# Output norms of the head groups: when the last scaling of a norm comes, and what the outgoing products wait for

## The chip, the cores and the metric

The kernel runs on one core of a Trainium2 chip. PE (TensorE) multiplies and transposes, DVE (VectorE), ACT (ScalarE) and POOL (GpSimd) work on elements, SP (SyncE) issues most of the transfers. Each engine takes its own instructions in the order in which the program records them, and waits for the others by semaphores. The metric is the time of one execution on the device in microseconds (us), as the median of several runs.

## The reference

One layer of a streaming encoder is computed for 1024 prompt tokens and 32 sample tokens. In the mix part, which the change touches, an input projection feeds two groups of heads: stick-breaking attention (8 heads of 64) and HGRN2 (4 heads of 128, a gated linear recurrence). Each head's output is normed on its own, and both go through one outgoing product:

```python
x = x + 0.5 * swiglu(rms_norm(x, ffn1_norm), ffn1_w_in, ffn1_w_out)
h = rms_norm(x, mix_norm)
sq, sk, sv, hq, hf, hi, hg = jnp.split(h @ w_in, IN_SPLIT_POINTS, axis=-1)
...
sb_o = rms_norm(sb_mix(sq, sk, sv), sb_out_gain).reshape(B, T, SB_WIDTH)
...
x = x + concat(normA(attnA), gatednormB(hgrnB)) @ w_out
x = x + 0.5 * swiglu(rms_norm(x, ffn2_norm), ffn2_w_in, ffn2_w_out)
```

(The last line but one is the docstring's wording; the sample tokens also read cached keys and values and a carried state.)

## The kernel before

Everything lies with channels on the 128 partitions and tokens along the row: T is 1056 columns, 1024 of the prompt and 32 of the sample, cut into three pieces of 384, 384 and 288 (TG is 384). A float32 product is made of three passes over high and low halves; `split` (L158 on ACT, L159 on DVE) makes these halves.

**The head groups.** Four head groups run one after the other, each of two attention heads and one HGRN2 head. For each there are three generators: `attend_stream` (prompt attention), `sample_stream` (attention of the 32 sample tokens) and `hg_stream` (the HGRN2 scan). A fourth generator, the products, runs beside all of them: first `project_stream` (L882, tile `pp`), the input projections of all groups, then `mix_stream` (L1520, tile `ps`), the outgoing products.

**What sets the order.** `merge` takes, again and again, the stream that stands at the earliest place and lets it record its next step. A step yields a cost; `Stream.advance` adds it up and turns the share of the stream's total (ATTEND_COST, SAMPLE_COST, HG_COST, or 412 units for the products) into a place. A stream that yields None waits, and the next one in line records a step. One unit of the products is six matmuls of a block. So the order of the instructions on every engine is fixed when the program is made; nothing is chosen on the chip, apart from what a scheduler of the program adds.

**Output norms.** Each head stream ends with a norm of its output, in blocks of TG columns, by `skewed`: first `factors` of block 0, then `factors` of block 1 and the scaling `normed` of block 0, and so on, with the last block's scaling alone at the end. `factors` squares the output on ACT (tile `sq`), transposes the squares on PE (`pmc`, L217), sums them per token and head on DVE (L218, tiles `fo` for attention and `fh` for the scan), and takes the power -1/2 on POOL (L224). `normed` spreads these factors over the rows again: for attention ACT widens them first (`wide`, L236), then PE transposes them (`pb`, L244), and DVE multiplies the output by them (L1096 for attention, tiles `so` and, for the sample tokens, `sos`). Prompt attention has three blocks, the scan three, the sample tokens one.

**Where outputs go.** In groups 0 to 2 the scaled output is stored to a DRAM tensor `mixd` (tiles c0, c1, c2 of it for attention and c4, c5, c6 for the scan); in group 3 it is split straight into operands (`xs_b`). `mix_stream` begins by loading the six tiles of `mixd` one after the other into `mraw` (L1481), in the two buffers `qn` and `kn` in turn (c0, c2 and c5 share one, c1, c4 and c6 the other), and splits each into `xs_a`. Its products then read `xs_a` in the order c0, c1, c2, c4, c5, c6. It may record these loads as soon as the last keys are done (`dup_done[3]`), once the projections have been recorded; a load of a part of `mixd` waits for the stores into it that were recorded ahead of it.

Of the kernel before, what the change touches and what calls it, by code (L numbers as in the profile page):

```python
# [1070 lines left out]
def skewed(first, second, items):  # L1071

    items = list(items)
    for i in range(len(items) + 1):
        if i < len(items):
            first(items[i])
            yield 1.0
        if i:
            second(items[i - 1])
            yield 0.5  # L1080


def sb_out_norm(g, pool, psp, o, w, out):
    nc = g.nc
    f = {}

    def factors(c):
        cw = min(TG, w - c)
        sq = g.wp.tile([P, TG], F32, name="sq", tag="xp", bufs=3)
        nc.scalar.activation(sq[:, 0:cw], o[:, c:c + cw], AF.Square)  # L1090
        f[c] = pool.tile([P, 3, 2], F32, name="fo", tag="fo", bufs=3)
        token_factors(g, f[c], psp, sq, cw, g.filler)

    def normed(c):
        cw = min(TG, w - c)
        nc.vector.scalar_tensor_tensor(out=o[:, c:c + cw], in0=o[:, c:c + cw], scalar=g.og[:, 0:1],  # L1096
                                       in1=spread(g, psp, f[c], 0, cw), op0=ALU.mult, op1=ALU.mult)
        out(c, c + cw, o[:, c:c + cw])

    yield from skewed(factors, normed, range(0, w, TG))  # L1100


def step_cost(w):
    return (w + 256) / 512.0


def attend_parts():

    for h in range(2):
        for p in range(4):  # L1110
            for a in ((0,) if p < 2 else (512, 0)):
                for i in (2 * p, 2 * p + 1):
                    yield h, p, a, i, min(a + 512, (i + 1) * P)


ATTEND_COST = sum(step_cost(e - a) for _, _, a, _, e in attend_parts()) + 12.0


def attend_stream(g, m, pool, psp, gi, out):
# [230 lines left out]
def hg_stream(g, m, pool, psp, hh, state, outs, out):  # L1350
# [108 lines left out]
    def normed(n):  # L1459
# [4 lines left out]
        out(*GROUPS[n], o[:, gs(n)])  # L1464

    yield from skewed(factors, normed, range(NG))
    m.scanned[hh] = True

# [5 lines left out]
def mix_stream(g, m, psp, xs, mix, xd):  # L1474

    nc = g.nc
    while not m.dup_done[3]:
        yield None
    for i, c in enumerate(MIX_FIRST):
        raw = m.sp.tile([P, T], F32, name="mraw", tag=("qn", "kn")[i % 2], bufs=1)  # L1480
# [147 lines left out]
def tile_layer(ctx: ExitStack, tc: tile.TileContext, *aps):  # L1628
# [207 lines left out]
    def products():  # L1836
        yield from project_stream(g, psp, xs_mix, jobs)
        m.projected = True
        yield from mix_stream(g, m, psp, xs_mix, mix, xd)

    def attention(gi):
        yield from attend_stream(g, m, m.sp, psp, gi, to_xs(3) if gi == 3 else to_dram(gi))
        finish()

    def sample(gi):
        yield from sample_stream(g, m, m.sp, psp, gi, ck, cv, to_xs(3) if gi == 3 else to_dram(gi))
        finish()
# [20 lines left out]
    for gi in range(4):  # L1868
        t0 = 7.0 * gi
        end = PLACES_END if gi == 3 else PLACES  # L1870
        streams.append(Stream(attention(gi), ATTEND_COST, *(t0 + t for t in end[0])))
        streams.append(Stream(sample(gi), SAMPLE_COST, *(t0 + t for t in end[1])))
# [103 lines left out]
```

## Time and profile before

| | |
|---|---|
| median of 3 runs | 2154.57 us (2151.69 to 2154.62) |
| the profiled execution's own time | 2158.07 us |
| its span, first to last instruction | 2156.4 us |
| mean granted TensorE clock | 0.996 |
| PE busy in 700 to 1450 us, where the head groups run | 735.50 of 750 us |
| head groups 0, 1, 2 end at about | 922, 1077, 1231 us |
| last input projection, last loads of `mraw` | about 1307 us, 1317 us |

The profile is of one execution. A group row gives the busy time of an engine and the mean of one instruction; a timeline row gives start and length, and in brackets how long the engine had stood idle before it and which instruction released it. In a row of stretches the last three numbers are the granted clock of TensorE, the share of the DMA engines, and GB/s.

### The profile page before, as it was taken

The page shows a single profiled execution, that of the slowest core. Times are in us where ns is not written, and L with a number is a line of the kernel's source. Part 1 is how long each engine was busy: PE and PEld are TensorE (multiplying, and loading weights), DVE is VectorE, ACT ScalarE, POOL GpSimd, SP SyncE. Part 2 cuts the span into 40 slices and gives each one's busy share as a digit, 9 for nine tenths or more (in the row PEclk, how much of TensorE's full clock was granted, in tenths as well). Part 3 has the DMA queues.
Part 4 walks back from the last instruction along what each step waited for, and adds up shares of the span by engine and source line. Part 5 has one row for each costly group of instructions (what it writes and reads, how often), then busy time and mean ns, then how long its engine had stood idle before and what let it go on. Part 6 is the DMA issues. An engine that isn't in the chain of part 4 may idle for free.

```text
span 2156.4 us, 41445 instructions
## 1 busy us (share of the span) xinstructions
PE 2107.1 (98%) x16331; PEld 2056.6 (95%) x16331; DVE 1470.4 (68%) x2546; ACT 937.8 (43%) x1820; POOL 590.7 (27%) x873
## 2 busy tenths in 40 slices
PE   7999999999999999999999999999999999999998
PEld 7999999999999999989899898999999999999998
DVE  5877666664678658778678688559677666645775
ACT  6433233233446555555564565246233233334443
POOL 1355544341000111311311311031565454320000
PEclk9999999999999999999999999999999999999999
DMA  7665555547535320120121122465765555566343
GB/s 230 188 204 176 156 166 168 160 140 265 204 123 169 117 59 21 44 70 21 55 60 29 60 68 92 147 192 160 226 210 173 165 164 162 165 231 231 120 144 125
DMA packets 327076, 305.12 MB, mean 141 GB/s; under 512 B 26400, under 2 KB 283168, under 8 KB 326880
## 3 DMA queue, kind: packets, MB, share of 16 engines
q1 hardware_dynamic: 257728, 262.59, 37.6%
q10 hardware_dynamic: 68672, 38.25, 6.2%
q8 instruction: 128, 2.10, 0.4%
q0 software_dynamic: 480, 1.62, 0.2%
q14 instruction: 68, 0.56, 0.1%
HBM read 207.37 MB, written 95.03 MB: 140 GB/s over the span
## 4 chain that ended last, share of the span: by engine, by line
PE 81%; DMA 7%; DVE 5%; POOL 2%; issue 2%; ACT 2%; SPq 0%; ACTq 0%; DVEq 0%; POOLq 0%
PE bk L431 33%; PE bk L746 20%; PE pp L882 14%; PE ps L1520 2%; PE pl L1391 2%; PE av L1158 1%; PE pt L1139 1%; DMA oraw<-in_ffn_w_out_dram 1%; DMA wraw<-in_ffn_w_in_dram 1%; DMA gd<-gt 1%; PE bk L799 1%; PE z L1194 1%; DMA p<-pd 1%; PE ps L1547 1%; PE z L1193 1%
## 5 line engine op out<-in xcount | busy, mean ns | idle before, releaser
L746 PE MATMUL bk<-tl,wh 128*128 128x256 f32 x1232 | 350.1, 285 | 1.0 <-DVE tl L704 0.9
L746 PE MATMUL bk<-th,wl 128*128 128x256 f32 x1232 | 349.2, 284 | 0.0
L746 PE MATMUL bk<-th,wh 128*128 128x256 f32 x1232 | 348.0, 284 | 0.7 <-ACT th L703 0.7
L882 PE MATMUL pp<-xs_a,wh 128*128 128x384 f32 (+1 forms) x1008 | 258.4, 338 | 0.0
L746 PEld LDWEIGHTS bk<-tl,wh 128*128 128x128 f32 x1232 | 231.8, 188 | 1.8 <-DVE tl L704 1.6
L746 PEld LDWEIGHTS bk<-th,wh 128*128 128x128 f32 x1232 | 230.9, 188 | 1.2 <-ACT th L703 1.0
L746 PEld LDWEIGHTS bk<-th,wl 128*128 128x128 f32 x1232 | 231.8, 188 | 0.2 <-issue 0.2
L882 PEld LDWEIGHTS pp<-xs_a,wh 128*128 128x128 f32 x1008 | 168.6, 189 | 6.1 <-issue 4.1
L693 DVE SCALAR_TENSOR_TENSOR wl<-oraw,wh 128x1024 fp32r<-128x1024 f32 x84 | 96.0, 1142 | 107.8 <-ACT wh L692 107.8
L882 PE MATMUL pp<-xs_a,wl 128*128 128x384 f32 (+1 forms) x504 | 163.9, 325 | 0.0
L586 POOL TENSOR_TENSOR gt<-gt,b 128x256 f32<-128x256 f32 x88 | 74.4, 846 | 316.4 <-ACT gt L585 316.4
L692 ACT ACTIVATE wh<-oraw 128x1024 fp32r<-128x1024 f32 x84 | 83.7, 997 | 148.6 <-PE bk L746 126.5
L159 DVE TENSOR_TENSOR wl<-wraw,wh 128x512 fp32r<-128x512 f32 (+2 forms) x126 | 110.7, 893 | 34.1 <-ACT wh L158 33.8
L585 ACT ACTIVATE gt<-gt 128x256 f32<-128x256 f32 x88 | 37.2, 423 | 219.3 <-DVE gt L552 219.2
L431 PE MATMUL bk<-ops_a,wh 128*128 128x256 f32 (+1 forms) x704 | 130.2, 285 | 2.2 <-ACT e L411 2.2
L158 ACT ACTIVATE wh<-wraw 128x512 fp32r<-128x512 f32 (+2 forms) x126 | 89.5, 731 | 91.2 <-PE bk L431 27.5
L590 POOL TENSOR_TENSOR gt<-gt,b 128x256 f32<-128x256 f32 x88 | 89.4, 1016 | 81.7 <-DVE b L552 69.1
L431 PEld LDWEIGHTS bk<-ops_a,wh 128*128 128x128 f32 x704 | 108.8, 188 | 2.8 <-ACT e L411 2.8
L552 DVE TENSOR_TENSOR gt<-bk,p 128x256 f32<-128x256 f32 (+1 forms) x60 | 25.9, 432 | 109.1 <-PE bk L431 106.3
L431 PE MATMUL bk<-ops_a,wl 128*128 128x272 f32 (+1 forms) x352 | 99.9, 285 | 0.3 <-DVE wl L159 0.3
L882 PEld LDWEIGHTS pp<-xs_a,wl 128*128 128x128 f32 x504 | 94.7, 188 | 0.1
L1050 ACT ACTIVATE t<-z,minus 128x128 f32<-128x128 f32 (+2 forms) x96 | 55.4, 577 | 62.8 <-PE z L1196 48.5
(437 smaller groups left out, 6559.5 us busy)
## 6 DMA issues: line engine op xcount, KB each, us to landing
wraw<-in_ffn_w_in_dram SPq DMA_DIRECT2D x58, 512.0 KB, 4.2
oraw<-in_ffn_w_out_dram SPq DMA_DIRECT2D x94, 256.0 KB, 4.6
sd<-osum SPq DMA_DIRECT2D x44, 512.0 KB, 3.1
gd<-gt SPq DMA_DIRECT2D x42, 528.0 KB, 5.0
braw<-in_ffn_w_in_dram ACTq DMA_DIRECT2D x42, 512.0 KB, 4.4
oraw<-sd SPq DMA_DIRECT2D x40, 512.0 KB, 3.8
oraw<-in_ffn_w_out_dram SPq DMA_DIRECT2D x30, 512.0 KB, 3.4
wraw<-in_w_in_dram SPq DMA_DIRECT2D x28, 512.0 KB, 3.7
```

The lines of the kernel that those rows point to most:

```text
L158: nc.scalar.activation(hi, src, AF.Copy)
L159: return nc.vector.tensor_tensor(out=lo, in0=src, in1=hi, op=ALU.subtract)
L431: mm = g.nc.tensor.matmul(ps, wt[x][:, kk, :], xt[y][:, kk, :], start=(first and kk == 0 and n == 0), stop=(kk == HK - 1 and n == len(PASS ...
L586: nc.gpsimd.tensor_tensor(out=gt[:, 1, cc], in0=gt[:, 1, cc], in1=s["b2"], op=ALU.mult)
L590: last = nc.gpsimd.tensor_tensor(out=gt[:, 0, cc], in0=gt[:, 0, cc], in1=s["b1"], op=ALU.mult)
L692: nc.scalar.activation(h, r, AF.Copy, scale=0.5)
L693: nc.vector.scalar_tensor_tensor(out=l, in0=r, scalar=0.5, in1=h, op0=ALU.mult, op1=ALU.subtract)
L746: nc.tensor.matmul(ps, wt[a][:, d * P:(d + 1) * P], xt[b][:, cols(c)], start=(k == 0 and n == 0), stop=(k == FH - 1 and n == len(PASSES) - 1))
L882: g.filler = nc.tensor.matmul(ps[:, 0:gw(n)], wt[a][:, k, :], xs(b, k)[:, gs(n)], start=(k == 0 and j == 0), stop=(k == KC - 1 and j == le ...
L1050: nc.scalar.activation(a, z, AF.Sigmoid, scale=minus)
L1391: nc.tensor.matmul(pl[0:rows, c, 0:hl].rearrange("p (b m) -> p b m", m=m_), k[:, cs(b, c)][:, 0:rows], qr, start=True, stop=True)
L1520: nc.tensor.matmul(ps[:, 0:w], wt[a][:, k, :], xs(b, c)[:, gs(n)], start=(k == 0 and i == 0), stop=(k == 5 and i == len(PASSES) - 1))
```

## The change

`skewed` gets one more step ahead of the last scaling: it yields 2.0 units, so that other streams record their steps first. ATTEND_COST grows by the same 2.0; the totals of the sample streams and of the scan stay as they were (10 and 24). `mix_stream` now waits, beside `dup_done[3]`, until all outputs of the first three groups have been recorded as done (`attended`, `sampled`, `scanned`).

```diff
@@ -1076,6 +1076,8 @@
             first(items[i])
             yield 1.0
         if i:
+            if i == len(items):
+                yield 2.0
             second(items[i - 1])
             yield 0.5
 
@@ -1113,7 +1115,7 @@
-ATTEND_COST = sum(step_cost(e - a) for _, _, a, _, e in attend_parts()) + 12.0
+ATTEND_COST = sum(step_cost(e - a) for _, _, a, _, e in attend_parts()) + 14.0
 
@@ -1474,7 +1476,7 @@
 def mix_stream(g, m, psp, xs, mix, xd):
 
     nc = g.nc
-    while not m.dup_done[3]:
+    while not (m.dup_done[3] and all(m.attended[:3] + m.sampled[:3] + m.scanned[:3])):
         yield None
```

No instruction of the computation is added or taken away. Lines behind 1078 stand two further down in the new kernel (L1520 becomes L1522, L1096 becomes L1098, and so on).

On PE at the end of head group 2, before (`pb<-identr,wide` belongs to prompt attention, `pb<-identr,fh` to the scan):

```order
L217 MATMUL pmc<-identr,sq 128x128 x3
L882 MATMUL pp<-xs_a,wh 128x384 x2
L882 MATMUL pp<-xs_a,wl 128x384
L882 MATMUL pp<-xs_b,wh 128x384
L244 MATMUL pb<-identr,wide 128x128 x3
L882 MATMUL pp<-xs_b,wh 128x384
L882 MATMUL pp<-xs_b,wl 128x384
L244 MATMUL pb<-identr,fh 128x128 x3
L882 MATMUL pp<-xs_a,wh 128x384
L244 MATMUL pb<-identr,wide 128x128 x2
```

And after the change, at the same place:

```order
L217 MATMUL pmc<-identr,sq 128x128 x3
L244 MATMUL pb<-identr,fh 128x128 x3
L217 MATMUL pmc<-identr,sq 128x128 x3
L1195 MATMUL z<-KH,Q 128x128
L244 MATMUL pb<-identr,fh 128x128 x3
L1196 MATMUL z<-KL,Q 128x128
L1198 MATMUL z<-cmask,identr 128x128
L882 MATMUL pp<-xs_a,wh 128x384 x2
L244 MATMUL pb<-identr,wide 128x128 x2
L882 MATMUL pp<-xs_a,wl 128x384
```

The attention's last `pb` stands further behind its `pmc`, and the scan's `pmc` and `pb` stand next to each other, with little between them.

On SP, where the outputs are loaded again, before (`mraw<-mixd` are the loads, `mixd<-sos` stores the sample tokens' scaled output of group 2, `xp` are tiles of the residual):

```order
L1481 DMA mraw<-mixd 128x1056
L1227 DMA craw<-in_cache_sb_k_dram 128x4x128
L1232 DMA vnew<-vsd 32x128
L1481 DMA mraw<-mixd 128x1056
L174 DMA wraw<-in_w_out_dram 128x3x128 x2
L1805 DMA mixd<-sos 128x32
L1481 DMA mraw<-mixd 128x1056 x2
L1487 DMA xp<-xd 128x384 x2
L1481 DMA mraw<-mixd 128x1056 x2
```

And after the change:

```order
L1483 DMA mraw<-mixd 128x1056
L1229 DMA craw<-in_cache_sb_k_dram 128x4x128
L1234 DMA vnew<-vsd 32x128
L1483 DMA mraw<-mixd 128x1056
L174 DMA wraw<-in_w_out_dram 128x3x128 x2
L1483 DMA mraw<-mixd 128x1056 x2
L1807 DMA mixd<-sos 128x32
L1489 DMA xp<-xd 128x384 x2
L1483 DMA mraw<-mixd 128x1056
L174 DMA wraw<-in_w_out_dram 128x3x128 x2
L1489 DMA xp<-xd 128x288
L1483 DMA mraw<-mixd 128x1056
```

The store of `sos` has moved behind the third and fourth load (these are now c4 and c6); the two loads behind it are c2, which it writes a part of, and c5.

On DVE after the change, from the scaling of `sos` on (L159 with `mraw` is the low half of a split; `hk`, `hq`, `att`, `hf` at L1403 to L1411 are a level of the scan of group 3):

```order
L159 TENSOR_TENSOR xs_a<-mraw,xs_a 128x1056
L159 TENSOR_TENSOR sbl<-pt,sbh 128x4x128
L1375 TENSOR_TENSOR att<-pd,identr 128x512
L1098 SCALAR_TENSOR_TENSOR sos<-sos,og,pb 128x32
...
L159 TENSOR_TENSOR xs_a<-mraw,xs_a 128x1056
L218 TENSOR_REDUCE fo<-pmc 128x6
L1403 TENSOR_TENSOR hk<-hk,hf 128x512
L1405 TENSOR_TENSOR hq<-hq,hf 128x512
L1410 COPY_PREDICATED att<-lmask_3097,pl 128x512
L1411 TENSOR_TENSOR hf<-hf 128x512
L159 TENSOR_TENSOR xs_a<-mraw,xs_a 128x1056
```

The scaling of `sos`, which stood ahead of every split of `mraw`, now comes behind the split of c4; the last row, c2's split, stands behind the four rows of the scan's level.

## The prediction, on record before the changed kernel was run

> **What bounds the kernel now.** I read the page's busy shares first, then the PE waits of the stretch between 730 and 1400 us in which the four head groups run, then the timelines of the places where the change moves something.
>
> ```profile
> PE 2107.1 (98%) x16331; PEld 2056.6 (95%) x16331; DVE 1470.4 (68%) x2546; ACT 937.8 (43%) x1820; POOL 590.7 (27%) x873
> ```
>
> PE is the bound: every other engine has a third of the span free. The change neither adds nor removes a matmul, so only PE's idle time (and its clock) can move the end. In the stretch that it touches, the largest waits of PE are these (total us, times, longest):
>
> ```profile
> PE pb L244 <- ACT wide L236: 4.2, 4, 1.5
> PE ps L1520 <- DVE xs_a L159: 1.1, 2, 0.7
> PE pmc L217 <- DVE fh L218: 0.6, 2, 0.3
> ```
>
> The first row is what the change aims at: `pb` spreads the token factors of an output norm over the rows, right before the last scaling of that norm. Three of the four are the ends of head groups 0, 1 and 2 (columns: start, us, instruction, idle before it):
>
> ```profile
> 922.29 0.44 PE L244 MATMUL pb<-identr,wide 128*128 128x128 f32 x2 [1.19 <-ACT wide L236]
> 1077.01 0.44 PE L244 MATMUL pb<-identr,wide 128*128 128x128 f32 x2 [1.51 <-ACT wide L236]
> 1231.40 0.44 PE L244 MATMUL pb<-identr,wide 128*128 128x128 f32 x2 [1.27 <-ACT wide L236]
> ```
>
> Together 3.97 us. That is little: 0.18% of the kernel, just under the 0.2% (4.3 us) that a measurement of this kernel can tell from no change. All else depends on what the move costs elsewhere.
>
> **Part 1: ends of groups 0 to 2.** The end of group 2, engine by engine:
>
> ```profile
> 1228.02 0.86 POOL L224 TENSOR_TENSOR fh<-fh,mh 128x3 f32<-128x3 f32 x1
> 1229.29 1.61 POOL L224 TENSOR_TENSOR fo<-fo,mh 128x4 f32<-128x4 f32 x1
> 1230.93 0.41 ACT L236 ACTIVATE wide<-fo 128x256 f32<-128x256 f32 x1 [3.94 <-POOL fo L224]
> ```
>
> POOL's power of the last `fo` ends at 1230.90, ACT widens it until 1231.34, PE goes on at 1231.40. With the attention's last `pb` behind some 5 us more of other products, this wait goes in all three groups: 4.0 us. Half of the `pmc` waits (0.6) go too: 0.3. But the scan's own norm uses the same helper, and there the order now sets `pmc` and its `pb` closer for the middle block. What that chain takes by itself stands at the end of group 3:
>
> ```profile
> 1406.32 0.55 PE L217 MATMUL pmc<-identr,sq 128*128 128x128 f32 x3 [0.98 <-ACT sq L1453]
> 1406.91 0.55 DVE L218 TENSOR_REDUCE fh<-pmc 128x3 f32<-128x384 f32 x1
> 1407.83 0.85 POOL L224 TENSOR_TENSOR fh<-fh,mh 128x3 f32<-128x3 f32 x1
> 1408.74 0.60 PE L244 MATMUL pb<-identr,fh 128*128 128x128 f32 x3 [0.74 <-POOL fh L224]
> ```
>
> `pmc` to `pb` needs 1408.74 - 1406.32 = 2.42 us. In the new order 1.0 to 1.4 us of PE work stands between the two, so about 1.05, 1.1 and 1.4 us of wait come up in the three groups, 3.55 in all. Net: 3.55 - 4.3 = **-0.7 us**. Bounds: -4.3 if other rows cover the new waits, +1.4 if only 0.5 us of work lies in each (3 x 1.9 - 4.3).
>
> **Part 2: the handoff to the outgoing products, around 1297 to 1340 us.** Here is the price. Sample attention of group 2 has one block only, so its only scaling is also its last: it is put off past the end of the projections. Now:
>
> ```profile
> 1298.16 0.24 DVE L1096 SCALAR_TENSOR_TENSOR sos<-sos,og,pb 128x32 f32<-128x32 f32 x1
> 1298.43 0.34 SPq L1805 DMA_DIRECT2D mixd<-sos  x1
> 1306.89 3.76 SPq L1481 DMA_DIRECT2D mraw<-mixd  x2
> 1317.03 1.45 SPq L1481 DMA_DIRECT2D mraw<-mixd  x2
> ```
>
> The store of `sos` leaves at 1298.43, long before the third load of `mraw` (output tile c2, into which `sos` goes) at 1306.89. In the new order DVE has the scaling behind the split of c4, and SP the store behind four loads; c2's load must wait for the store, and c5's load for c2's slot. I lay this chain out on the clock of the trace.
>
> ```profile
> 1310.00:1320.00 10.00, 9.30 (x61) 7.85 (x59) 9.91 (x14) 6.06 (x12) 0.91 (x4) 1.00 0.49 157
> mraw<-mixd SPq DMA_DIRECT2D x6, 528.0 KB, 3.3
> mixd<-sos SPq DMA_DIRECT2D x3, 16.0 KB, 1.4
> L158 ACT ACTIVATE xs_a<-mraw x6: 1074/1087/1119, 1303.8 to 1322.8; 128x1056 fp32r<-128x1056 f32 x6
> L159 DVE TENSOR_TENSOR xs_a<-mraw,xs_a x6: 1247/1255/1259, 1305.6 to 1323.9; 128x1056 fp32r<-128x1056 f32 x6
> ```
>
> (The first row gives the busy time of PE, PEld, DVE, ACT and POOL in a stretch: DVE is busy for 9.91 of its 10 us, so nothing on it comes early.) From the first split at 1305.6 on, the rows of DVE up to and with the scaling sum to 15.7 us, and I allow 1 us of waiting for PE: scaled at 1322.35. Store issued and landed (0.34 + 1.4, with some 0.2 between): 1324.3. c2 loaded (3.3): 1327.7. ACT's half of the split (1.09): 1328.9. DVE's half stands behind four rows of the scan's first level:
>
> ```profile
> 1329.90 0.70 DVE L1401 TENSOR_TENSOR hk<-hk,hf 128x512 f32<-128x512 f32 x1
> ...
> 1332.33 0.72 DVE L1409 TENSOR_TENSOR hf<-hf 128x512 f32<-128x512 f32 x1
> ```
>
> These take 3.1 us, so with 1.26 of its own it ends at 1331.2 to 1332.4; I take the later. Then c5: load to 1335.8, ACT to 1336.95, DVE to 1338.2. Until PE reaches the first low-half product of c5 it has, from 1305.68 on (behind the row at 1305.28), 19.7 us of rows at the pitches of the trace (0.175 us for a 384 wide product): without waits 1325.4. So PE idles for 12.8 us in this stretch. Before, eight waits stand there, the first and the last of them:
>
> ```profile
> 1309.28 0.47 PE L1193 MATMUL z<-KH,Q 128*128 128x512 f32 x1 [0.64 <-DVE t L1054]
> ...
> 1336.57 0.55 PE L244 MATMUL pb<-identr,wide 128*128 128x128 f32 x3 [0.26 <-ACT wide L236]
> ```
>
> With 0.46, 0.28, 0.20, 0.67, 0.36 and 0.36 between them they sum to 3.2 us. Extra: **+9.6 us**. Bounds: +6, if DVE takes c2 as soon as ACT is done and `sos` is scaled 1.5 us earlier; +13, if both loads land in the 4.6 us that is the longest of the six in the trace. The parts of the wait that I get are 1.3 us ahead of a `z`, then 2.3 ahead of the attention's second `pmc`, 3.0 at c2's low half, 2.8 at c5's high half, and 0.9 or less elsewhere.
>
> **The clock.** What a wait of this length does beside itself:
>
> ```profile
> 1607.53 0.38 PE L431 MATMUL bk<-ops_b,S4l 128*128 128x256 f32 x1 [1.52 <-DVE S4l L159]
> 1607.00:1608.00 1.00, 0.47 (x4) 0.47 (x5) 0.81 (x2) 0.01 (x1) 0.91 (x1) 0.99 0.06 17
> 1608.00:1609.00 1.00, 1.00 (x7) 1.00 (x6) 0.76 (x3) 0.00 (x0) 0.88 (x2) 0.50 0.07 30
> 1611.00:1612.00 1.00, 1.00 (x9) 1.00 (x8) 1.00 (x3) 0.09 (x1) 0.00 (x0) 0.80 0.74 235
> 1492.98 0.51 PE L431 MATMUL bk<-ops_a,wh 128*128 128x256 f32 x2 [1.94 <-ACT e L411]
> 1494.00:1496.00 2.00, 2.00 (x19) 2.00 (x18) 1.97 (x3) 1.15 (x4) 0.00 (x0) 1.00 0.71 208
> ```
>
> After 1.52 us of idle PE the granted clock (third number from the end, ahead of the DMA share and rate) is 0.50 from 1608 on and back within 1611 to 1612: some 3.4 us. Seven matmuls a microsecond run there in place of the 9.5 that the row at 1494 shows, so one such dip loses about 3.4 x (1 - 7 / 9.5) = 0.9 us. After 1.94 us it did not come. The waits of 2.3, 3.0 and 2.8 us may each bring one; the first two would be hidden in the wait that follows them, the last not. I take one, **+0.9 us**; bounds 0 and +3.
>
> [...]
>
> **Part 3: end of group 3, 1396 to 1409 us.** Beside the 0.98 and 0.74 us quoted above:
>
> ```profile
> 1396.01 0.54 PE L244 MATMUL pb<-identr,fh 128*128 128x128 f32 x3 [0.58 <-POOL fh L224]
> 1405.41 0.52 ACT L158 ACTIVATE xs_b<-hf 128x384 fp32r<-128x384 f32 x1 [7.29 <-DMA x<-xd]
> ```
>
> ACT had stood for 7.29 us behind its own fetches of `x`, which made `sq` late. In the new order the `sq` of the last block stands ahead of these fetches, and 3 us of outgoing products lie between its `pmc` and `pb`. Gone: 0.58 + 0.98 + 0.74 = 2.3 us; I leave 0.5 for the splits of the last weights, which come later now. **-1.8 us**, bounds -2.3 and +0.5.
>
> **The sum:** -0.7 + 9.6 + 0.9 - 1.8 = +8.0 us. Against the profiled execution's own 2158.07 us that is 2166.1; this execution is 3.5 us above the median of the runs shown (2154.57), so for a median I say 2154.57 + 8.0 = **2162.6 us**.
>
> **Rivals.** *The handoff is covered* (0.25): sample's scaling comes through early enough that c2's and c5's loads meet PE with little wait; for it speaks that PE idles only 3.2 us there now though six loads pass through two slots in 20 us. Then +2 for the handoff and -2.5 for parts 1 and 3: 2154 us, no change. It decides if the scaling is done before about 1312 us, 10 us sooner than I place it; DVE's 9.91 of 10 speaks against it. *Faster* (0.10): the chain of POOL's power and ACT's widening was all that PE lost at the ends; the 4.0 us of `pb` waits and the 2.3 us of the tail go, nothing new comes up, since the scan's 2.42 us chain is filled by neighbouring rows and the handoff costs what it did. 2154.57 - 6.3 = 2148.3. It needs both the cover of the first rival and 2.4 us of work between each `pmc` and `pb`, where I count 1.0 to 1.4. *Worse* (0.05): both loads land late and the clock dips three times: 9.6 + 3.4 + 3 - 2.5 = 13.5, 2168 us. *The new wait does nothing*: that holds only if all stores of the first three groups have been issued when the projections end; the order shows the `sos` store behind four loads of `mraw`, so the wait has something to wait for. It belongs to the first rival.
>
> **How the numbers follow.** Forecast 0.60, the rivals as above. The forecast's own range is 2154 to 2168: the ends of its terms (6 - 4.3 - 2.3 = -0.6 at the bottom, 13 + 1 + 1.4 + 0.5 = 16 at the top) with the last 2.5 us of the top left out, where every term would have to go wrong at once. The range reaches down to 2150 to take in the first rival, and leaves out the faster one and the worst top, less than 2 in 10. Slower by more than 0.2%: 0.55 + 0.05 = 0.60; within: 0.23 from the first rival and 0.05 from the low end of the forecast, 0.28; faster: 0.12.
>
> **What would show it.** Right: PE waits at `ps` for `xs_a` of 5 us or more in all, the load of c2 after the `sos` store and over 15 us later than now, PE waits `pb <- POOL fh` of about 1 us at the ends of groups 0 to 2, none of 1.2 to 1.5 for `wide`. A dip of the granted clock between 1335 and 1345 us would bear out its term. Wrong: `sos` scaled well before 1320 us, or fewer than 6 us of PE idle between 1305 and 1345.

## The result and the profile after

| | before | after |
|---|---|---|
| median of 6 runs | 2154.60 us (2151.69 to 2157.07) | 2175.00 us (2168.91 to 2180.90) |
| ratio after / before, 95% interval | | 1.0092 (1.0081 to 1.0104) |
| the profiled execution's own time | 2158.07 us | 2177.00 us |
| its span, its mean granted clock | 2156.4 us, 0.996 | 2175.3 us, 0.991 |

The change makes the kernel slower by some 20 us; forecast were 8.0 us, with a range that ended at 2168.0. The direction was right, the size was not.

The first thing to read is the page's line of busy times of the changed kernel:

```profile
PE 2117.2 (97%) x16331; PEld 2064.8 (95%) x16331; DVE 1471.2 (68%) x2546; ACT 937.7 (43%) x1820; POOL 586.6 (27%) x873
```

PE runs the same 16331 matmuls, and yet it is busy for 10.1 us longer than before (2117.2 - 2107.1). The profile lists the idle time ahead of an instruction apart from its busy time: so part of the loss is not idle time at all, but slower work. The other part is in PE's waits, here those of 730 to 1480 us of the changed kernel (total us, times, longest):

```profile
PE pb L244 <- POOL fh L224: 4.4, 3, 2.0
PE pl L1393 <- DVE att L1410: 3.1, 3, 1.3
PE pmc L217 <- ACT sq L1092: 2.8, 3, 1.8
PE z L1195 <- DVE t L1054: 2.8, 4, 1.2
PE ps L1522 <- DVE xs_a L159: 2.6, 2, 1.9
PE ps L1549 <- DVE x L1552: 2.1, 2, 1.7
```

The row that stood at the top, `pb <- ACT wide`, has fallen from 4.2 to 1.0 us. In its place are the same `pb` for the scan's factors (`fh`), a level of the scan (`pl`), the attention's scan (`z`), and waits of the outgoing products. Three of the long ones inside the groups, in the timeline of PE; the first two rows are ends of head groups, the third is in the middle of one:

```profile
918.46 0.54 PE L244 MATMUL pb<-identr,fh 128*128 128x128 f32 x3 [1.47 <-POOL fh L224]
1233.11 0.77 PE L244 MATMUL pb<-identr,fh 128*128 128x128 f32 x3 [2.04 <-POOL fh L224]
1012.92 1.30 PE L1393 MATMUL pl<-hq,hk 128*128 128x64 f32 x10 [1.25 <-DVE att L1410]
```

What follows two of them is in the 1 us stretches (granted clock third from the end):

```profile
1012.00:1013.00 1.00, 0.07 (x1) 0.11 (x1) 1.00 (x2) 1.00 (x4) 0.00 (x0) 1.00 0.00 0
1014.00:1015.00 1.00, 1.00 (x11) 0.93 (x9) 0.07 (x1) 0.00 (x0) 0.00 (x0) 0.91 0.00 0
1015.00:1016.00 1.00, 1.00 (x5) 0.94 (x5) 1.00 (x2) 0.00 (x0) 0.00 (x0) 0.50 0.03 8
1018.00:1019.00 1.00, 1.00 (x8) 0.97 (x7) 0.73 (x2) 0.00 (x0) 0.00 (x0) 0.88 0.00 0
...
1232.00:1233.00 1.00, 0.00 (x0) 0.00 (x0) 1.00 (x3) 0.00 (x0) 0.92 (x2) 1.00 0.00 0
1233.00:1234.00 1.00, 0.89 (x5) 0.89 (x6) 1.00 (x3) 0.00 (x0) 0.36 (x3) 0.64 0.00 0
1236.00:1237.00 1.00, 1.00 (x7) 1.00 (x6) 0.36 (x1) 0.41 (x2) 0.00 (x0) 0.66 0.26 83
```

Behind a wait of 1.25 us and behind one of 2.04 us the granted clock is 0.50 for some 3.4 us: in 1014 to 1015 PE runs 11 matmuls, in the next microsecond 5. While PE is the bound, 0.50 of the clock for 3.4 us is 1.7 us of time, an estimate from these rows. Summed over all 1 us stretches between 700 us and the first product behind the mix part, before lost nothing in this way, and the changed kernel 13.6 us: eight such dips, from about 1015, 1172, 1233, 1332 (10.24 us without a break, counted as three), 1346 and 1445 us on. PE's waits of 0.15 us and more in the same stretch sum to 14.1 us before and 23.9 after. So +9.8 us of idle PE and +13.6 us of clock, 23.4 in all, and the stretch got 22.4 us longer: 2.2 us of PE's idle time lie inside the dip from 1332.26 to 1342.50 us, and 0.50 of them, 1.1 us, stand in both numbers. Ahead of the stretch the profiled execution after is 1.7 us faster than the one before, and behind it it gains 1.9 us more, which leaves the 18.9 us between the spans.

The handoff to the outgoing products has four of the eight dips. Its transfers on SP's queue, PE's waits and the 5 us stretches of the changed kernel:

```profile
1315.79 11.13 SPq L1483 DMA_DIRECT2D mraw<-mixd  x2
1327.89 0.32 SPq L1807 DMA_DIRECT2D mixd<-sos  x1
1330.99 0.32 SPq L1483 DMA_DIRECT2D mraw<-mixd  x1
1339.46 0.34 SPq L1483 DMA_DIRECT2D mraw<-mixd  x1
```

```profile
1331.59 0.55 PE L217 MATMUL pmc<-identr,sq 128*128 128x128 f32 x3 [1.77 <-ACT sq L1092]
1339.49 0.69 PE L1522 MATMUL ps<-xs_a,wh 128*128 128x384 f32 x1 [1.93 <-DVE xs_a L159]
1343.85 0.62 PE L1522 MATMUL ps<-xs_a,wh 128*128 128x384 f32 x2 [0.99 <-ACT xs_a L158]
1345.15 0.44 PE L1522 MATMUL ps<-xs_a,wh 128*128 128x384 f32 x1 [0.68 <-DVE xs_a L159]
```

```profile
1330.00:1335.00 5.00, 3.41 (x19) 3.41 (x19) 3.08 (x5) 1.94 (x3) 3.58 (x4) 0.73 0.83 252
1335.00:1340.00 5.00, 2.79 (x11) 1.73 (x11) 4.74 (x10) 1.08 (x1) 0.52 (x1) 0.50 0.15 43
1340.00:1345.00 5.00, 3.48 (x12) 2.85 (x10) 2.33 (x5) 1.61 (x2) 0.36 (x2) 0.75 0.32 108
1345.00:1350.00 5.00, 4.85 (x22) 4.85 (x23) 1.21 (x3) 0.42 (x1) 0.00 (x0) 0.66 0.20 75
```

(The first row of SP holds two loads, c4's at 1315.79 and c6's at 1326.58.) The store of `sos` leaves at 1327.89, 29 us later than before. The load of c2 follows at 1330.99, its low half meets PE at 1339.49, and the load of c5 leaves only then.

To see in which part the time was lost, I matched the products one by one (the k-th matmul of `pp` or `ps` before and after). The cut at 1350 us is good to some 1.5 us, since other work stands between the products there in another order:

| part (times of before) | predicted | measured | PE's waits before, after | clock lost |
|---|---|---|---|---|
| groups 0 to 2, up to 1299 us | -0.7 | +9.5 | 7.7, 12.1 | 5.1 |
| handoff, 1299 to 1350 | +9.6 and +0.9 of clock | +9.4 | 3.8, 8.5 | 6.8 |
| behind it, up to 1457 | -1.8 | +3.5 | 2.6, 3.4 | 1.7 |

The handoff came out near the forecast in total, with less idle time and more lost clock than forecast. What was missed lies on both sides of it.

### The profile page after: what moved, and what is told of

Same layout as the page of the kernel before. It is cut to its first block, busy times and chain, and to the rows that moved or that the text cites. A ratio compares the mean times of both kernels' runs of the same rounds, so it can differ in the third digit from the quotient of the medians.

```text
span 2175.3 us, 41448 instructions
## 1 busy us (share of the span) xinstructions
PE 2117.2 (97%) x16331; PEld 2064.8 (95%) x16331; DVE 1471.2 (68%) x2546; ACT 937.7 (43%) x1820; POOL 586.6 (27%) x873
## 4 chain that ended last, share of the span: by engine, by line
PE 83%; DVE 5%; DMA 5%; issue 3%; ACT 2%; POOL 2%; ACTq 0%; SPq 0%; DVEq 0%; POOLq 0%
PE bk L431 35%; PE bk L746 19%; PE pp L882 14%; PE ps L1522 2%; PE pl L1393 2%; PE av L1160 2%; PE pt L1141 1%; DMA x<-xd 1%; DMA gd<-gt 1%; PE pmc L217 1%; PE z L1195 1%; DMA gt<-pd 1%; PE z L1196 1%; DVE t L1052 1%; PE bk L799 1%
## 5 line engine op out<-in xcount | busy, mean ns | idle before, releaser
L159 DVE TENSOR_TENSOR wl<-wraw,wh 128x512 fp32r<-128x512 f32 (+2 forms) x126 | 110.7, 894 | 29.1 <-ACT wh L158 27.9
L882 PE MATMUL pp<-xs_b,wh 128*128 128x384 f32 (+1 forms) x336 | 82.2, 324 | 0.0
```

The source lines that it names most:

```text
L159: return nc.vector.tensor_tensor(out=lo, in0=src, in1=hi, op=ALU.subtract)
L882: g.filler = nc.tensor.matmul(ps[:, 0:gw(n)], wt[a][:, k, :], xs(b, k)[:, gs(n)], start=(k == 0 and j == 0), stop=(k == KC - 1 and j == le ...
```

## The experiments

All kernels are compared with the kernel before in runs on the same chip. The us column is the ratio times 2154 us.

| label | what it is | ratio (95% interval) | us |
|---|---|---|---|
| e1_cost_only | before, ATTEND_COST + 2 | 1.0029 (1.0020 to 1.0038) | +6 |
| e2_yields_cost12 | before, all three last scalings late | 1.0093 (1.0071 to 1.0115) | +20 |
| e3_sample_late | before, the sample tokens' alone | 1.0057 (1.0039 to 1.0075) | +12 |
| e4_attention_scan_late | before, attention's and scan's | 1.0034 (1.0022 to 1.0047) | +7 |
| e5_attention_late | before, attention's alone | 1.0035 (1.0023 to 1.0047) | +8 |
| e6_scan_late | before, scan's alone | 1.0002 (0.9992 to 1.0011) | 0 |
| e7_c2_last | after, c2 loaded and used last | 1.0059 (1.0042 to 1.0077) | +13 |
| e8_pe_kept_busy | after, products that nobody reads in the handoff | 1.0107 (1.0090 to 1.0125) | +23 |
| e9_sample_not_late | after, the sample tokens' scaling not late | 1.0016 (1.0006 to 1.0025) | +3 |
| e10_no_new_wait | after, c2's load ahead of the `sos` store | 1.0031 (1.0018 to 1.0044) | +7 |
| e11_pe_kept_busy_at_c5 | as e8, split otherwise | 1.0104 (1.0089 to 1.0119) | +22 |
| e12_cost_11 | before, ATTEND_COST - 1 | 1.0055 (1.0036 to 1.0074) | +12 |
| e13_longer_wait | before, work added to POOL | 1.0008 (0.9998 to 1.0017) | +2 |
| e14_twice_as_long | before, twice as much | 0.9997 (0.9989 to 1.0006) | -1 |
| e15_long_but_busy | e14, and transposes added to PE | 1.0031 (1.0020 to 1.0042) | +7 |
| e16_chain_longer_by_3 | before, three more steps on `fo` | 1.0022 (1.0013 to 1.0030) | +5 |
| e17_chain_longer_by_6 | before, six more | 1.0048 (1.0033 to 1.0063) | +10 |
| e18_chain_6_but_busy | e17, PE kept busy in the wait | 1.0071 (1.0056 to 1.0085) | +15 |

### One part of the change at a time: e1 to e6, e9

`skewed` got a third argument, and each of its callers (attention, sample tokens, scan) its own value:

```diff
-def skewed(first, second, items):
+def skewed(first, second, items, late=0.0):
...
         if i:
+            if late and i == len(items):
+                yield late
             second(items[i - 1])
```

e2 gives 2.0 to all three and leaves ATTEND_COST at 12, e3 to e6 give it to the callers named in the table, e1 to none but sets ATTEND_COST to 14. e9 is the whole change without the sample tokens' 2.0. The new wait of `mix_stream` is in all of them. By itself it leaves the order of every engine as it was before, so there is nothing of it to run alone. The theories were: the handoff (late `sos`) carries nearly all of it; or the ends of groups do; or the constant does, since it shifts the places of the whole attention stream.

> ATTEND_COST 14 as in the change, no later scaling anywhere; nothing is left out of the computation. Theory A (the constant moves every step of attention to an earlier place and brings the stalls inside groups 1 and 2, each with a dip of the clock): the waits of about 1.2 us of pl for att near 1013 and 1170 us are there, with dips behind them, handoff with few waits, time 5 to 12 us above the kernel before. Theory B (the recorded prediction: the constant only balances the added step, the sample tokens' late scaling is what costs): within 3 us of the kernel before.

> All last scalings late as in the change, ATTEND_COST back at 12; nothing is left out. Theory A: the stalls of groups 1 and 2 are gone, the handoff keeps its waits and its dips, so about 10 to 13 us above the kernel before less some 3 us of gains at the ends of the groups: +7 to +12. Theory B: as the whole change, +15 to +20.

> Only the sample tokens' scaling is late, ATTEND_COST 12; nothing is left out. Both theories: the store of sos behind the third load of mraw, waits of PE for xs_a at the handoff of 4 us or more and dips behind them, +8 to +13 us. If the handoff only costs together with the constant: under +4 us.

> Last scalings of attention and of the scan late, the sample tokens' not, ATTEND_COST 12; nothing is left out. Theory A: neither the constant's stalls nor the handoff's, the three waits for wide gone, time 0 to 5 us below the kernel before. Theory B: new waits of pb for fh at the ends of the groups eat the gain, within 2 us of the kernel before or above it.

> Only the prompt attention's last scaling late, ATTEND_COST 12; nothing is left out. Theory A (the scan's own late scaling puts its pmc and pb side by side and brings the waits of 1.8 to 2.1 us for fh of run e4): no wait for wide and none of that length for fh at the ends of groups 0 to 2, time 2 to 5 us below the kernel before. Theory B (the late end of attention holds up the next group's attention, which starts only then): waits for t and sbl near 1243 to 1256 us as in e4, time 2 to 6 us above the kernel before.

> Only the scan's last scaling late, ATTEND_COST 12; nothing is left out. Theory A: the loss of e4 (some +7) sits here, +4 to +8. Theory B: within 2 us of the kernel before, the waits for wide as before.

> The whole change with ATTEND_COST 14, but the sample tokens' scaling not late; nothing is left out. Runs so far: the constant alone +6, attention and scan late at cost 12 +7, the sample tokens late alone +12, the whole change +20. If the constant does what it is put there for and makes up for the added step: its +6 goes, and +7 to +8 is left (whole change less the 12 of the sample tokens). If all parts simply add: +13. The theory of the record (only the sample tokens cost) would have -2.

The late sample scaling is the largest part: +12 us alone, and the whole change without it costs only +3. But the constant alone costs +6 and the late attention scaling alone +8, where I had reckoned with nothing and with a gain.

**The constant (e1).** Written out as an order of some 12,300 rows, with line numbers left aside, e1 differs from before on PE in about 1000 rows (those gone and those new counted), the whole change in about 1200, and the late scaling of the scan in under 60. A larger total makes each yield of the attention count for a smaller share, so every step of the attention moves to an earlier place, not the last one alone. What this does is in e1's timeline of PE, and in that of DVE just ahead:

```profile
1008.78 1.41 PE L1393 MATMUL pl<-hq,hk 128*128 128x64 f32 x11 [1.45 <-DVE att L1410]
1163.39 1.93 PE L1393 MATMUL pl<-hq,hk 128*128 128x64 f32 x15 [1.24 <-DVE att L1410]
```

```profile
1004.12 1.28 DVE L1052 TENSOR_TENSOR_SCAN t<-t,left,zero 128x512 f32<-128x512 f32 x1 [1.30 <-ACT t L1050]
1005.54 0.69 DVE L1054 TENSOR_TENSOR t<-z,t 128x512 f32<-128x512 f32 x1
1006.15 0.69 DVE L1403 TENSOR_TENSOR hk<-hk,hf 128x512 f32<-128x512 f32 x1
```

The scan's level (`hk` and the rows behind it) now stands behind a step of the attention for which DVE itself waits 1.30 us; the wait for `att` before was 0.44 us at this place. Behind the second of the two waits of PE the clock falls to half from 1165 us on. The profiled execution of e1 (2155.59 us) is the fastest of its ten: +1.3 us of idle and one dip, 3 us. What fills the other 3 us of the median's +6 has no trace.

**The late attention scaling (e5, and e4 with it).** The `wide` waits at the ends of groups are gone here, as the change intends. In their place, e5 at the end of group 2, on PE and on POOL:

```profile
1233.15 0.60 PE L244 MATMUL pb<-identr,fh 128*128 128x128 f32 x3 [1.86 <-POOL fh L224]
```

```profile
1229.00 0.86 POOL L224 TENSOR_TENSOR fh<-fh,mh 128x3 f32<-128x3 f32 x1
1230.27 1.61 POOL L224 TENSOR_TENSOR fo<-fo,mh 128x4 f32<-128x4 f32 x1
1231.97 0.20 POOL L223 TENSOR_SCALAR fh<-fh 128x3 f32<-128x3 f32 x1
1232.25 0.85 POOL L224 TENSOR_TENSOR fh<-fh,mh 128x3 f32<-128x3 f32 x1
```

The power of the attention's `fo` still takes its 1.61 us on POOL, ahead of the scan's last `fh`. Only now PE waits for the second instead of the first, which ends a little later: 1.77, 2.10 and 1.86 us at the three ends, 5.7 in all, where `wide` had cost 4.0. In group 3 the attention starts later too, and PE waits 1.07 us for a scan of it (`z <- t`) and twice 0.6 us for rows that come behind a low half `sbl`. Two of the three long waits brought a dip. Idle +4.1 and two dips of 1.7: 7.5 us, as measured.

This is e5's order, and not that of the whole change. There, with ATTEND_COST at 14, POOL has long done the power of `fo` when the scan's factors come: at the end of group 2 it starts at 1226.46 and takes 1.01 us, and PE's wait of 2.04 us ends at 1233.11. What PE waits for there is told below, with part 1 of the prediction.

**The late scan scaling (e6)** costs nothing by itself, and the `wide` waits stay as they were. It is no test of the closeness of the scan's `pmc` and `pb`, which was my reason for new waits at the ends of groups: in e6's order products of `pp` still stand between the middle block's `pmc` and `pb`, and at the end of group 2 PE's longest wait for `fh` is 0.22 us.

The parts don't add up: e1 and e4 are +6 and +7, and together (e9) they make +3. Each moves the places of all streams, and what waits for what is worked out anew. e12, with the constant one smaller, shows the same from the other side:

> The kernel before with ATTEND_COST 11 in place of 12, no late scaling; nothing is left out. e1 showed that 14 puts a scan of attention ahead of the first level of HGRN2 on DVE and costs +6. If the loss comes from attention being too early: with 11 it comes later, the waits of pl for att (0.44 us) shrink, 0 to 3 us below the kernel before. If 12 is simply a point at which the rows fit and any move costs: +2 to +8.

It costs +12 us, more than the two units up, and its trace has no dip between 700 and 1450 us, so this loss is not one of the clock. The change of total is no small matter in either direction.

### The handoff: e7, e10, e8, e11

e7 keeps the whole change, but loads and multiplies c2, the tile that waits for the store, as the last of the six:

```diff
+MIX_ORDER = (0, 1, 4, 5, 6, 2)
...
-    for i, c in enumerate(MIX_FIRST):
+    for i, c in enumerate(MIX_ORDER):
...
-        for k, c in enumerate(MIX_FIRST):
+        for k, c in enumerate(MIX_ORDER):
```

e10 takes the new wait of `mix_stream` out again, so that c2 is loaded ahead of the store of `sos`. The 32 sample columns of c2 of group 2 then are not those of the reference: an earlier store, of group 1, puts a value there.

```diff
-    while not (m.dup_done[3] and all(m.attended[:3] + m.sampled[:3] + m.scanned[:3])):
+    while not m.dup_done[3]:
         yield None
...
+            if c == 1 and a == TP:
+                nc.sync.dma_start(mix[2, :, a:e], o)
```

> The whole change, with the six tiles loaded and multiplied in the order c0, c1, c4, c5, c6, c2; nothing is left out. If the handoff's loss is the chain store of sos, load of c2, load of c5 into its slot: PE then has four more tiles of products before it needs c2, waits for xs_a under 2 us, fewer dips there, time 6 to 12 us below the whole change. If it is the crowded DVE and ACT alone: within 3 us of the whole change.

> The whole change without its third edit: the outgoing products' loads do not wait for the sample tokens of group 2. Their 32 columns of c2 are then loaded ahead of their store (an earlier store of group 1's puts a value there), so these columns of the output differ. If the chain over the store of sos is the handoff's loss: c2 and c5 loaded early, waits for xs_a under 2 us, 6 to 12 us below the whole change, as e7. If not: within 3 us of it.

Both bear the chain out. In e7, PE waits only for the last tile:

```profile
1336.02 0.62 PE L1523 MATMUL ps<-xs_a,wh 128*128 128x384 f32 x2 [1.69 <-ACT xs_a L158]
1337.32 0.44 PE L1523 MATMUL ps<-xs_a,wh 128*128 128x384 f32 x1 [0.68 <-DVE xs_a L159]
```

Its products lose some 2 us between 1299 and 1350 us of before, against 9.4 with c2 in its old place, and the kernel is some 7 us faster than the whole change (+13 for +20). In e10 the handoff has no wait for `xs_a` over 0.7 us and no dip; the kernel is at +7. So by the medians, of the 20 us of the whole change 13 hang on the wait of c2 for the late store and what comes behind it, and 7 on the order of the groups.

In e8 and e11, 24 products whose result nobody reads stand between those of c1 and c2 and between those of c4 and c5 (12 and 12, and 8 and 16), to keep PE busy while the loads run:

```diff
+            if u == 0 and k in (2, 4):
+                idle = psp.tile([P, 512], F32, name="idle", tag="px", bufs=3)
+                for r in range(12):
+                    nc.tensor.matmul(idle[:, 0:TG], wt[0][:, 0, :], xs(0, 0)[:, 0:TG], start=True, stop=True)
```

> The whole change with 24 more products of 128x384 in the handoff whose result nobody reads (12 ahead of the second pmc, 12 ahead of the products of c2), 4.2 us of work for PE at full clock; nothing is left out of the computation. If idle PE is what brings the dips of the clock there: fewer dips between 1330 and 1350 us, and 2 to 5 us less than the whole change in spite of the added work. If the clock falls for another reason: the dips stay and the time is 0 to 4 us above the whole change.

> As e8, with the products that nobody reads placed anew: 8 ahead of the second pmc, 16 behind the products of c2, so 4.2 us of added work; nothing is left out of the computation. e8 still had a wait of 2.5 us at c5. If idle PE brings the dips: none between 1330 and 1350 us but for one at most, clock lost there under 2 us in place of 6.8, and the time 2 to 5 us below the whole change. If the dips stay: 0 to 4 us above it.

Neither is faster than the change, and neither decides what it was made for. A long wait stayed in both, in e8 this one:

```profile
1340.99 1.01 PE L1526 MATMUL ps<-xs_a,wh 128*128 128x384 f32 x2 [2.47 <-ACT xs_a L158]
```

With 24 products (4.2 us at 0.175 us) the handoff's dips fell from four to two, and the end didn't come earlier (+23 and +22 us, for +20). This fits a stretch whose end is set by the chain of transfers; that a slower PE mostly fills there what would be a wait is my estimate, from the 4.7 us of added idle time beside 6.8 us of lost clock in the changed kernel.

### What a wait costs beside itself: e13 to e18

In the groups PE is the bound (busy for 735.50 of 750 us before), and there the question is open: does a dip come from the wait ahead of it, and is it worth 1.7 us? The kernels take before with its order unchanged and make the `wide` wait at the ends of groups 0 to 2 longer. e13 and e14 put one and two multiplications of 128 x 256 on POOL ahead of the power, e15 has e14's and 24 transposes of the identity on PE ahead of the `pb`:

```diff
+    if slow:
+        for _ in range(1):
+            nc.gpsimd.tensor_tensor(out=sq[:, 0:256], in0=sq[:, 0:256], in1=sq[:, 0:256], op=ALU.mult)
     nc.gpsimd.tensor_scalar(out=v, in0=v, scalar1=nh / P, scalar2=EPS, op0=ALU.mult, op1=ALU.add)
```

> The kernel before with one more multiplication of 128x256 on POOL (its result read by nobody) ahead of the power of the attention's last block in groups 0 to 2; order of all other instructions as before, nothing left out. The waits for wide (1.2 to 1.5 us) grow by its length, some 0.85 us, to about 2.1. If a wait of PE costs only itself: 3 x 0.85 = +2.5. If waits of 2 us bring a dip of the clock in most cases (8 of the 10 such waits in the runs so far), each worth 1.7 us: +2.5 + 3 x 0.8 x 1.7 = +6.6, and the profile shows dips near 922, 1077 and 1231 us.

> As e13 with two such multiplications: waits of about 3 us. If a wait costs only itself: +5. If each brings a dip of 1.7 us: +5 + 5 = +10, a dip behind each of the three waits in the profile.

> As e14, and PE has 24 more transposes of the identity (result read by nobody, some 0.09 us each, 2.2 us) right ahead of each of the three waiting transposes: the chain is as long as in e14, but PE idles only some 0.8 us of it. If idle PE brings the dips: none there, +4 to +6, that is 3 to 6 us under e14. If the dips have another reason, or cost nothing: within 1 us of e14.

These three miss their aim: the multiplications hang on nothing of the chain, POOL did them in time that it had free, and in e13 and e14 the waits stayed at 1.2, 1.5 and 1.3 us. What e15 shows is that filling doesn't pay here. Its transposes hold PE for 2.62 us each time, 7.9 in all (the expectation of e18 takes 2.35), and took 4.0 us of waits away: 3.9 us more, and up to 1299 us of before its products take 4.3 us longer in the trace. By the medians the kernel got 7 us slower (4.3 to 9.0). In e16 to e18 the added steps work on `fo` itself, so that the power can't start ahead of them:

```diff
+    if slow:
+        for _ in range(3):
+            nc.gpsimd.tensor_scalar(out=v, in0=v, scalar1=1.0, scalar2=0.0, op0=ALU.mult, op1=ALU.add)
```

e17 has six of them, e18 six and e15's transposes.

> In e13 and e14 the added POOL work slid into POOL's own idle time ahead of the chain, and the three waits stayed at 1.2 to 1.5 us; so they told nothing. Here three more steps on the factors themselves (times 1 plus 0, some 0.28 us each) stand in the chain ahead of the power of the attention's last block, groups 0 to 2; nothing is left out. The three waits grow by some 0.85 us to about 2.1. If a wait costs only itself: +2.5. If 8 of 10 such waits bring a dip worth 1.7 us: +6.6.

> As e16 with six steps: the waits grow by 1.7 us to about 3. If a wait costs only itself: +5. If each brings a dip of 1.7 us: +10, with a stretch of granted clock 0.50 behind each of the three waits in the profile.

> As e17, and PE has 24 transposes of the identity that nobody reads (2.35 us in e15) right ahead of each of the three waiting transposes: the chain is as long as in e17, PE idles some 0.7 us of it. If idle PE brings the dips and they cost 1.7 us each: no dips there, +5 to +7, that is 3 to 5 us under e17. If the dips cost nothing or come for another reason: as e17 or above it.

The waits of e17 on PE, and the clock behind the first:

```profile
922.89 0.69 PE L247 MATMUL pb<-identr,wide 128*128 128x128 f32 x2 [2.86 <-ACT wide L239]
1081.92 0.44 PE L247 MATMUL pb<-identr,wide 128*128 128x128 f32 x2 [2.88 <-ACT wide L239]
1239.41 0.44 PE L247 MATMUL pb<-identr,wide 128*128 128x128 f32 x2 [2.91 <-ACT wide L239]
```

```profile
922.00:923.00 1.00, 0.11 (x1) 0.12 (x2) 0.00 (x0) 0.42 (x1) 0.83 (x3) 0.78 0.00 0
923.00:924.00 1.00, 1.00 (x4) 1.00 (x5) 0.39 (x1) 0.00 (x0) 0.60 (x1) 0.50 0.00 0
...
928.00:929.00 1.00, 1.00 (x4) 1.00 (x4) 0.00 (x0) 0.51 (x2) 0.00 (x0) 0.50 0.07 16
929.00:930.00 1.00, 1.00 (x6) 1.00 (x6) 0.00 (x0) 0.00 (x0) 0.00 (x0) 0.81 0.07 16
```

The three waits grew by 4.7 us in all (8.65 for 3.97), and the kernel by 10.3 us (7.1 to 13.6): more than the waits alone give. In the traces the products take 10.6 us longer up to 1299 us of before. All three brought a dip, the first a double one: 3.4 + 1.7 + 1.7 = 6.8 us of clock in the profiled execution. e16: waits of 2.03, 2.06 and 2.09 us, +2.2 in all, two dips, and +4.7 us (2.8 to 6.5). So of the six waits of 2.03 to 2.91 us in e16 and e17, at a place where PE is the bound, five had a dip behind them, and beside the added length the kernels lost a further 2.5 us for the two dips of e16 and 5.6 us for the 6.8 us of clock of e17, by the medians.

In e18 PE's waits fell to 1.52, 1.01 and 1.59 us and the dips in this stretch from four to one, which ties the dips to the idle time. But the kernel is not faster than e17. The transposes hold PE for 2.78 us each time here, 8.3 in all, and take 3.5 us of waits and 5.1 us of dips away: 0.3 us less by this sum, 0.6 us more in the products of the two traces up to 1299 us. So in the traced stretch the sum closes to 1 us. By the medians e18 is 4.5 us slower than e17; the rest of that lies outside of this stretch or in executions without a trace (e18's has a dip at 1613 us that e17's has not), and stays open.

## Why the prediction was wrong in size

**The chain of the handoff: right.** It was laid out for the scaling of `sos`, its store, c2's load, the split's two halves, then c5. The products stand 7.6 us later at 1299 us than before, so the predicted 1332.4 and 1338.2 us become 1340.0 and 1345.8; PE got c2's low half at 1339.49 and c5's at 1345.15. On the way the steps are off by up to 2 us (the scaling was done about 2 us sooner, c2's load issued 3.1 us behind the store and landed 4.4 us later). One of the named signs did not show: PE's waits for `xs_a` sum to 3.9 us, where 5 or more were expected. The rival that it is covered is out: `sos` is scaled at 1327.6, not before about 1312.

**The clock: right in kind, wrong in price and number.** "I take one, +0.9 us" was worked out from matmuls per microsecond of rows with other shapes. The clock itself gives it straight: 0.50 of it for 3.4 us is 1.7 us, and e17 bears that price out (10.6 us in the products, for 4.7 us of added waits and 6.8 us of clock). And I looked for dips in the handoff alone, where they are half hidden: its idle time grew by only 4.7 us instead of 9.6, beside 6.8 us of lost clock, and by my estimate PE at a clock of 0.50 filled the rest. In the groups, where PE is the bound, I had none; three came.

**Part 1, -0.7 us: the step that failed.** The ends of the groups, for which it was laid out, came out. The `wide` waits there are gone, and in their place PE waits for the scan's factors `fh`: 1.47, 0.87 and 2.04 us, 4.4 in all where 3.55 were reserved. The chain of the last of them, on PE and on POOL:

```profile
1229.80 0.55 PE L217 MATMUL pmc<-identr,sq 128*128 128x128 f32 x3
```

```profile
1231.03 1.09 POOL L223 TENSOR_SCALAR fh<-fh 128x3 f32<-128x3 f32 x1 [1.47 <-DVE fh L218]
1232.20 0.85 POOL L224 TENSOR_TENSOR fh<-fh,mh 128x3 f32<-128x3 f32 x1
```

From `pmc` to the `pb` at 1233.11 it takes 3.31 us, as in group 0; in group 1 it takes the 2.42 us of the forecast. The difference is POOL's multiply-and-add, 1.09 us in place of 0.20. All waits of PE for `pmc` and `pb` at the three ends sum to 4.9 us before and 4.4 after: -0.5, near the -0.7 of part 1.

What failed is that these ends were taken for the whole of the groups, and that the term of the clock looked at the handoff alone: inside the groups the change was put at nothing. PE's waits there went from 2.8 to 7.7 us. Those for `att` grew from 1.3 to 3.1 us (two of 1.25 and one of 0.62), and one of 0.88 us for a `z` came at 1256.93; both come with ATTEND_COST alone, too (e1: 1.45, 1.24, 0.62 and 0.89). It was not priced at all: I treated the two units as the counterpart of the step they pay for, while they shift the place of every attention step. Another 2.7 us of waits came near 990 and 1147 us; they stand in e10 as well and not in e9, so they go with the sample tokens' late scaling. And three dips add 5.1 us of clock, two behind the `att` waits and one behind the 2.04 us. So 4.4 us of waits and 5.1 us of clock make the 9.5 of the table, where -0.7 was forecast.

**Part 3, -1.8 us.** The three old waits (0.58, 0.98 and 0.74 us) are gone, as forecast. But behind the late handoff others come. The timelines of PE and DVE after:

```profile
1443.51 0.39 PE L1549 MATMUL ps<-xs_b,lh 128*128 128x256 f32 x1 [1.74 <-DVE x L1552]
```

```profile
1443.03 0.42 DVE L1552 TENSOR_TENSOR x<-ps,x 128x256 f32<-128x256 f32 x1 [2.99 <-DMA x<-xd]
```

DVE waits for a fetch of `x`. These fetches are issued by ACT from 1417.7 to 1439.3 us, before from 1392.2 to 1418.3: 21 to 26 us later, while the products are 14 to 22 us later. A dip follows at 1445. In e10, where the handoff isn't held up, neither the old waits nor new ones over 0.3 us stand here. But the delay alone doesn't explain it: e7, whose handoff loses little, has such a wait of 1.90 us, and e8 and e11, whose handoff is held up as here, have none. What brings it stays open.

**The sum.** Of the 14.4 us by which the stretch of the profiled pair (22.4) misses the forecast (8.0), 10.2 are part 1 and 5.3 part 3, and the handoff with its clock gives 1.1 back. That the handoff's total fits is in part luck: too much idle time and too little clock were forecast. The range was too narrow at the top for one reason above all: the bounds of part 1 (-4.3 to +1.4) held the ends of the groups alone. Its top also took 1 us for the clock, where the term's own bound was 3; but with 3, and with nothing left out, it would have ended at 2172.5, still below the measured 2175.0.

**The spread.** The six executions of the changed kernel go from 2168.91 us at a mean clock of 0.995 to 2180.90 us at 0.989, and 0.006 of 2175 us is 13 us, about what lies between them. So the clock lost differs from one execution to the next; by what, no run here shows.

## What to carry to other kernels

Where a merge of streams is steered by totals, a total that is changed along with one step moves all steps of its stream: compare the whole order and price that shift by itself, before the step. When a wait is taken away, look at the queue of the engine that was waited for and name the next one who stands behind the same instruction (e5). Don't take the places at which a change aims for all the places that it moves. And price a new wait of PE, where PE is the bound, at its length and a possible dip of the clock of 1.7 us, unless something else sets the end there: in the traces here 10 of 49 waits of 1.15 to 1.55 us and 13 of 16 of 2.0 us or more had such a dip.

## What was not expected of the hardware

The granted clock of 0.50, for 3.41 us at a time, behind waits of 0.8 to 3 us. Over the profiled executions of all 20 kernels (700 to 1450 us, waits inside a dip left out), a dip began during, or within 3 us of the end of, 13 of 16 waits of PE of 2.0 us or more, of 5 of 13 between 1.55 and 2.0 us, of 10 of 49 between 1.15 and 1.55 us, and of 2 of 43 between 0.8 and 1.15 us; no dip stood without such a wait.

The length of the wait doesn't decide alone, and the traces show a second thing beside it. In each of them all dips ahead of 2140 us start on one grid with steps of 3.413 us, which is also the length of a single dip in the changed kernel: its dips at 1171.84, 1233.28, 1332.26, 1345.91 and 1444.90 us are 46, 64, 93, 97 and 126 steps behind the one at 1014.82. Cut a trace into the cells of its grid and add up PE's idle time in each (700 to 1450 us, cells inside a dip left out): a dip began with the next cell behind all 17 cells that have 1.86 us or more of it, behind 10 of 37 with 1.24 to 1.85 us, and behind 1 of 4310 with less. The 2.04 us at the end of group 2 lie in one cell after the change, and a dip followed. The 2.05 us at the same place in e9 and e10 lie across two cells (1.36 and 0.69 us, 0.50 and 1.54), and none followed. What sets the grid, and what decides between 1.24 and 1.85 us, no run here shows.

On POOL, a power of 128 x 4 numbers took 1.01 us in one place of the changed kernel (1226.46) and 1.61 us in another kernel with the same line (e5, 1230.27), and a multiply-and-add of 128 x 3 took 0.20 and 1.09 us a few microseconds apart:

```profile
1226.46 1.01 POOL L224 TENSOR_TENSOR fo<-fo,mh 128x4 f32<-128x4 f32 x1
...
1228.42 0.20 POOL L223 TENSOR_SCALAR fh<-fh 128x3 f32<-128x3 f32 x1 [0.38 <-DVE fh L218]
1231.03 1.09 POOL L223 TENSOR_SCALAR fh<-fh 128x3 f32<-128x3 f32 x1 [1.47 <-DVE fh L218]
```

What DVE does beside the last of them:

```profile
1230.86 1.26 DVE L1052 TENSOR_TENSOR_SCAN t<-t,left,zero 64x512 f32<-64x512 f32 x1
```

Both end at 1232.12. In the 20 traces this step of `fh` and `fo` took over 0.4 us in 77 of 605 cases, and each of the 77 ended within 0.08 us of the end of a DVE instruction (140 of the other 528 did); all 29 that began while DVE ran a scan are among them. Why these steps are longer, and why the end of a DVE instruction goes with it, no run here shows. The power of 1.61 us in e5 stands beside three rows of DVE, the one of 1.01 us beside none; what decides there stays open, too.
